# Recurrence of an RWKV branch: scaled keys of both groups of heads ahead of their products, products deferred and bound together

## The chip, the cores and the metric

The kernel runs on one core of one Trainium2 chip. Its time is the device time of one launch in microseconds (us). The engines are TensorE (PE in the profile, its weight loads PEld), VectorE (DVE), ScalarE (ACT), GpSimd (POOL) and SyncE (SP), of which the last only issues transfers here. GpSimd's queue issues transfers too.

## The reference: what is computed

The reference runs two transformer blocks in float32 over 512 tokens of width 1024. The first block has an attention layer and a recurrent layer; the change lies in the recurrent layer. This layer multiplies its normed input (512 latent and 256 context tokens) by `rec_w_in`, runs an RWKV branch (8 heads of 64) and a long-convolution branch ("hyena") beside each other, and multiplies both, gated, by `rec_w_out`. The RWKV branch, cut and condensed to what matters:

```
def rwkv_features(u, w0, w_up, a0, a_up, k_k, k_a):
    r, k, v, dw_f, dw_b, da_f, da_b = split_cols(u, RWKV_SPLITS)
    kk = normalised(k * k_k)                                  # per head
    for d, (dw, da) in enumerate(((dw_f, da_f), (dw_b, da_b))):   # two directions
        w_log = -softplus(-(w0[d] + tanh(dw) @ w_up[d])) - 0.5
        decay = exp(-exp(w_log));  a = sigmoid(a0[d] + da @ a_up[d])
        k_d = k * (1 + (a - 1) * k_a);  b_d = kk * a

def wkv_scan(s0, r, decay, k, v, kk, b, reverse, emit):
    def step(s, inp):
        r_t, w_t, k_t, v_t, kk_t, b_t = inp
        sa = einsum('bhij,bhj->bhi', s, kk_t)
        s = s * w_t[:, :, None, :] - sa[..., None] * b_t[:, :, None, :] + v_t[..., None] * k_t[:, :, None, :]
        y = einsum('bhij,bhj->bhi', s, r_t) if emit else None
        return s, y
```

The scan runs forward and backward, over the context first and then from its state over the latent tokens; the two results are added, normalised per head (`rwkv_readout`), and a bonus term r * k * r_k * v is added.

## The kernel before, in words

It is written in a tile language: pools with a number of buffers per name, and a scheduler that sets each engine's order from priorities (the place in the program, moved by `high_priority`) and from what is ready by its own estimate. Waits between engines, and for a buffer's last reader, follow from that. So the written order is not the built order, and both matter below.

The scan is done in windows of 128 tokens, two of context and four of latent tokens, each for both directions d at once (direction 1 runs through the windows from the other end), in two groups h of four heads, and in two chunks of 64 tokens per window. For each window there are these pieces of work:

- `decays(o, d, h)`, four times a window: TensorE's "lora" products (line 1153, `mm<-lora,wu`) into a tile of the pool mm2, which has one buffer; ScalarE's tanh into `ta` and `G` (1159); GpSimd's `kd` and `G` (1162, 1164); VectorE's running sum over G (1166); ScalarE's exponentials; GpSimd's kd product; for latent windows a store of kd from SyncE's queue (1176); VectorE's ta (1177), KR, and the scaled keys kT (1184), by the tiles ta, kd and G. `ta` has one buffer, `kd` and `G` have two, `kT` one for each direction.
- `products(o, d, h, kT)`, four times a window: eight products of keys (1198, `mm<-KR,kT`) into another tile of the same mm2 buffer; ScalarE takes N from it (lines 1206 and 1208), VectorE AK (1211) and, in latent windows, DD (1213); then four transposes of kT on TensorE into the PSUM tile "tr" (1219), which ScalarE copies to kn (1220).
- `invert`: VectorE's inversion of all four N of the window, 62 small operations between the transposes 1321 and 1336, and products on TensorE behind it (1351, 1353).
- `steps(o, c, VU)`: the recurrence over one chunk (lines 1387 to 1415), a chain through TensorE, VectorE and ScalarE.

`prep(o, h)` is two decays and then two products, of one group of heads. The loop over the six windows i writes: steps of chunk 0 of window i, inversion of window i + 1, steps of chunk 1, prep of window i + 2 for h = 0 and then h = 1, values of window i + 1.

Around this chain the scheduler lays work that is independent of it: `late()` is `values()` (products of the weights for v and r), `rest()` (the weight products for the gates and the convolution's inputs; priorities set by `at` as fractions of the stage), `rwkv_bonus`, `conv` (the convolution; its first lines, the transform's tables `tab` (1623) and its spectrum `K` (1644), are loaded by SyncE), and `rwkv_out` (normalisation of the result, lines 1479 to 1490, in two halves). Weight products (lines 114 to 116) take three TensorE products per block, with the weights split into a high and a low part: `wraw` is loaded by SyncE, ScalarE makes `whi` (108), VectorE `wlo` (109). Behind the stage stand the products with `rec_w_out`, whose weights go the same way. `hl` and `yl` (2472) are the low parts of their other factor.

## Time and profile before

| | |
|---|---|
| Median of 3 runs | 2869.42 us (2861.07 to 2869.76) |
| The profiled execution's own time | 2864.4 us |
| Its span in the trace | 2861.5 us |
| Mean granted TensorE clock | 0.951 |
| TensorE busy | 2645.9 us, 92% of the span |
| VectorE busy | 1495.3 us, 52% |
| ScalarE busy | 1028.4 us, 36% |
| GpSimd busy | 503.8 us, 18% |

A row of the table by windows gives a stretch in us from the start of the span, then the busy time of each engine in it with its number of instructions, then the granted clock of TensorE (1.00 is full speed), the busy share of the DMA engines and GB/s. A row in order of time gives the start, the duration, engine, line, operation, out<-in, shapes and count; in square brackets stands the idle time of the engine just before it and what released it. A row by line gives busy time, mean duration in ns, and the idle time ahead with its releasers. TensorE's products overlap their neighbours in the pipeline, so their durations add up to more than the time between their starts. The recurrence's stage lies between 755 and 1290 us of the span.

### The profile page before, as it was taken

The page shows a single profiled execution, that of the slowest core. Times are in us where ns is not written, and L with a number is a line of the kernel's source. Part 1 is how long each engine was busy: PE and PEld are TensorE (multiplying, and loading weights), DVE is VectorE, ACT ScalarE, POOL GpSimd, SP SyncE. Part 2 cuts the span into 40 slices and gives each one's busy share as a digit, 9 for nine tenths or more (in the row PEclk, how much of TensorE's full clock was granted, in tenths as well). Part 3 has the DMA queues.
Part 4 walks back from the last instruction along what each step waited for, and adds up shares of the span by engine and source line. Part 5 has one row for each costly group of instructions (what it writes and reads, how often), then busy time and mean ns, then how long its engine had stood idle before and what let it go on. Part 6 is the DMA issues. An engine that isn't in the chain of part 4 may idle for free.

```text
span 2861.5 us, 43340 instructions
## 1 busy us (share of the span) xinstructions
PE 2645.9 (92%) x16642; PEld 2125.4 (74%) x16642; DVE 1495.3 (52%) x3219; ACT 1028.4 (36%) x2165; POOL 503.8 (18%) x803
## 2 busy tenths in 40 slices
PE   8998998989989889878999998999989999899998
PEld 5897445678767666658888877777868776888887
DVE  4144557736487888685344237762232566444423
ACT  4223335524344444223333224432222663323322
POOL 1011001222343332432000001311010344100000
PEclk9999899989899899988999998999987999999999
DMA  6111431142223332524333323232453315233332
GB/s 231 60 60 55 145 119 63 57 129 81 83 87 113 90 93 66 174 94 138 96 96 96 96 85 108 83 96 91 122 160 104 106 55 161 89 100 100 96 96 88
DMA packets 251018, 290.60 MB, mean 102 GB/s; under 512 B 17415, under 2 KB 197082, under 8 KB 250812
## 3 DMA queue, kind: packets, MB, share of 16 engines
q1 hardware_dynamic: 239292, 251.29, 28.4%
q0 software_dynamic: 10704, 33.41, 3.9%
q8 instruction: 131, 2.15, 0.3%
q10 hardware_dynamic: 816, 3.15, 0.3%
q14 instruction: 75, 0.61, 0.1%
HBM read 247.38 MB, written 35.68 MB: 99 GB/s over the span
## 4 chain that ended last, share of the span: by engine, by line
PE 71%; DVE 11%; issue 5%; POOL 5%; DMA 4%; ACT 3%; SPq 0%; DVEq 0%; POOLq 0%; ACTq 0%
PE mm L114 13%; PE mm L115 13%; PE mm L116 13%; PE gt L114 3%; PE gt L115 3%; PE gt L116 3%; PE ac L116 1%; PE ac L115 1%; PE ac L114 1%; PE ac L874 1%; PE fx L333 1%; PE ac L2053 1%; PE mm L813 1%; DVE wlo L109 1%; PE tr L857 1%
## 5 line engine op out<-in xcount | busy, mean ns | idle before, releaser
L109 DVE TENSOR_TENSOR wlo<-wraw,whi 128x512 fp32r<-128x512 f32 (+1 forms) x390 | 374.5, 961 | 690.1 <-ACT whi L108 683.3
L108 ACT ACTIVATE whi<-wraw 128x512 fp32r<-128x512 f32 (+1 forms) x390 | 323.7, 831 | 792.5 <-PE mm L115 224.3
L114 PE MATMUL mm<-hh,whi 128*128 128x512 f32 (+1 forms) x1024 | 384.0, 376 | 1.0 <-ACT hh L178 0.7
L115 PE MATMUL mm<-hl,whi 128*128 128x512 f32 (+1 forms) x1024 | 383.5, 375 | 0.0
L116 PE MATMUL mm<-hh,wlo 128*128 128x512 f32 (+1 forms) x1024 | 383.0, 374 | 0.1
L114 PEld LDWEIGHTS mm<-hh,whi 128*128 128x128 f32 x1024 | 193.8, 190 | 35.7 <-ACT hh L178 1.3
L116 PEld LDWEIGHTS mm<-hh,wlo 128*128 128x128 f32 x1024 | 193.5, 189 | 35.2 <-DVE wlo L109 1.2
L115 PEld LDWEIGHTS mm<-hl,whi 128*128 128x128 f32 x1024 | 193.9, 189 | 33.1
L114 PE MATMUL mm<-whi,mh 128*128 128x512 f32 (+1 forms) x480 | 172.4, 360 | 1.4 <-DVE th L2270 1.4
L115 PE MATMUL mm<-wlo,mh 128*128 128x512 f32 (+1 forms) x480 | 173.0, 360 | 0.1
L116 PE MATMUL mm<-whi,ml 128*128 128x512 f32 (+1 forms) x480 | 172.7, 360 | 0.0
L114 PE MATMUL gt<-hh,whi 128*128 128x512 f32 (+1 forms) x320 | 128.7, 402 | 7.0 <-ACT whi L108 6.4
L116 PE MATMUL gt<-hh,wlo 128*128 128x512 f32 (+1 forms) x320 | 128.3, 401 | 0.8 <-DVE wlo L109 0.8
L115 PE MATMUL gt<-hl,whi 128*128 128x512 f32 (+1 forms) x320 | 127.6, 399 | 0.0
L283 POOL TENSOR_TENSOR ss<-sq 128x1 f32<-128x1 f32 x8 | 1.6, 201 | 707.3 <-ACT th L277 707.3
L114 PE MATMUL mm<-lath,whi 128*128 128x512 f32 (+1 forms) x280 | 116.4, 417 | 0.1
L116 PE MATMUL mm<-lath,wlo 128*128 128x512 f32 (+1 forms) x280 | 113.7, 407 | 1.0 <-DVE wlo L109 1.0
L115 PE MATMUL mm<-latl,whi 128*128 128x512 f32 (+1 forms) x280 | 113.3, 405 | 0.4 <-DVE latl L179 0.4
L114 PEld LDWEIGHTS mm<-whi,mh 128*128 128x128 f32 x480 | 89.9, 188 | 15.8 <-DVE th L2270 1.8
L115 PEld LDWEIGHTS mm<-wlo,mh 128*128 128x128 f32 x480 | 90.1, 188 | 14.4 <-DVE wlo L109 0.8
L116 PEld LDWEIGHTS mm<-whi,ml 128*128 128x128 f32 x480 | 90.1, 188 | 13.8
L114 PEld LDWEIGHTS gt<-hh,whi 128*128 128x128 f32 x320 | 62.2, 194 | 21.7 <-ACT whi L108 7.4
(732 smaller groups left out, 5987.7 us busy)
## 6 DMA issues: line engine op xcount, KB each, us to landing
wraw<-in_ffn_w_gate SPq DMA_DIRECT2D x44, 512.0 KB, 3.5
wraw<-in_ffn_w_up SPq DMA_DIRECT2D x44, 512.0 KB, 3.6
wraw<-in_ffn_w_down SPq DMA_DIRECT2D x44, 512.0 KB, 3.7
wraw<-in_w_in SPq DMA_DIRECT2D x60, 256.0 KB, 2.8
wraw<-in_rec_w_in SPq DMA_DIRECT2D x58, 256.0 KB, 2.8
wraw<-in_attn_w_in SPq DMA_DIRECT2D x26, 512.0 KB, 3.7
ada_w<-in_rec_ada_w SPq DMA_DIRECT2D x24, 512.0 KB, 3.7
wraw<-in_w_branch_gate SPq DMA_DIRECT2D x48, 256.0 KB, 3.0
```

The source lines that it names most:

```text
L108: nc.scalar.activation(hi, raw, AF.Copy)
L109: self.weng.tensor_sub(lo, raw, hi.bitcast(F32))
L114: mm(out, lh, rh, start=start, stop=False)
L115: mm(out, lh, rl, start=False, stop=False)
L116: mm(out, ll, rh, start=False, stop=stop)
L283: nc.gpsimd.tensor_add(ss, sq[:, i, 0:1], sq[:, i, 1:2])
L333: nc.tensor.matmul(p[o:o + 32], self.cs[:, kk], w[:, k], start=kk < 4, stop=kk >= 4, tile_position=(0, o))
L813: nc.tensor.matmul(ps[p][:, o:o + n], qaT[heads[p], pr, 128 * i:128 * i + 128], ks[p], start=True, stop=True)
L857: nc.tensor.transpose(t[:, j * 128:j * 128 + 128], s[:, a:a + 128], b.ident)
L874: nc.tensor.matmul(o[heads[p], xs], va[rows, n, h * 64:h * 64 + 64], pT[rows, p, j, xs], start=j == 0, stop=j == nk - 1)
L2053: nc.tensor.matmul(o, r["v"][br][:, j], pT[br][:, j].rearrange("p a b -> p (a b)"), start=False, stop=br == 1 and j == i)
```

## The change

Of the two groups of heads of a window, all four `decays` are written first, and then all four `products`; before, each group's two products stood behind its own two decays. In `products`, the first of the eight key products is given a later place (`late_by`, 0.6 of the priorities that one turn of the loop takes; 0 for the first two windows), and the other seven and the four transposes are bound to follow it on TensorE (`issue_after`), with the priority set back. The tiles change with it: kT gets two buffers per direction, kd one instead of two, and the raw weights of `values()` two instead of three. The line numbers behind this place shift by 9 or 10.

```diff
-        with tc.tile_pool(name="rv_w", bufs=1, side="right") as work, b.weights(side="right", size=512):
+        with tc.tile_pool(name="rv_w", bufs=1, side="right") as work, b.weights(raw=2, side="right", size=512):
...
-            kd = wp.tile([128, 2, H], F32, name="kd", bufs=2)
+            kd = wp.tile([128, 2, H], F32, name="kd")
...
-            kT = wp.tile([128, 2, 2, 2, 64], F32, name=f"kT{d}")
+            kT = wp.tile([128, 2, 2, 2, 64], F32, name=f"kT{d}", bufs=2)
...
+            todo = list(itertools.product(range(2), repeat=3))
+            with tc.high_priority(offset=-late_by[0]):
+                first = part(*todo[0])
+            kn = w3.tile([128, 2, 2, 128], F32, name=f"kn{d}")
+            pt = b.psum(512, "tr")
+            with tc.high_priority(offset=late_by[0]), tc.issue_after(first.ins):
+                for x in todo[1:]:
+                    part(*x)
+                for c in range(2):
+                    for pr in range(2):
                         m = 2 * c + pr
...
+                        nc.tensor.transpose(pt[:, m * 128:m * 128 + 128], kT[:, pr, c].rearrange("p x t -> p (x t)"), b.ident)
...
-        def prep(o, h):
+        def scaled(o, h):
...
-            kT = [decays(o, d, h) for d in range(2)]
-            for d in range(2):
-                products(o, d, h, kT[d])
+            return [decays(o, d, h) for d in range(2)]
+
+        def prep(o):
...
+            kT = [scaled(o, h) for h in range(2)]
+            for h in range(2):
+                for d in range(2):
+                    products(o, d, h, kT[h][d])
...
         for i in range(6):
+            q0 = tc.cur_priority
...
-            prep_of(i + 2, 0)
-            prep_of(i + 2, 1)
+            late_by[0] = int(0.6 * (tc.cur_priority - q0))
+            prep_of(i + 2)
```

TensorE's built order in the first window, from the lora products of the second round of decays on (x4 stands for four instructions of the kind in a row, mm_7437 and so on are tiles of mm2 or of weight products), before:

```order
L1153 MATMUL mm_7437<-lora,wu 128x128 x4
L115 MATMUL mm<-latl,whi 128x512
L116 MATMUL mm<-lath,wlo 128x512
L114 MATMUL mm<-lath,whi 128x512
L115 MATMUL mm<-latl,whi 128x512
L116 MATMUL mm<-lath,wlo 128x512
L114 MATMUL mm<-lath,whi 128x512
L1219 MATMUL tr<-ident,kT_7429 128x128 x4
L115 MATMUL mm<-latl,whi 128x512
L116 MATMUL mm<-lath,wlo 128x512
L1198 MATMUL mm_7462<-KR_7427,kT_7429 128x64 x8
```

and after:

```order
L1153 MATMUL mm_7437<-lora,wu 128x128 x4
L115 MATMUL mm<-latl,whi 128x512
L116 MATMUL mm<-lath,wlo 128x512
L114 MATMUL mm<-lath,whi 128x512
L115 MATMUL mm<-latl,whi 128x512
L116 MATMUL mm<-lath,wlo 128x512
L114 MATMUL mm<-lath,whi 128x512
L115 MATMUL mm<-latl,whi 128x512
L116 MATMUL mm<-lath,wlo 128x512
L114 MATMUL mm<-lath,whi 128x512
L115 MATMUL mm<-latl,whi 128x512
L1153 MATMUL mm_7469<-lora,wu 128x128 x4
```

Before, the transposes of the first round's keys and their products stand six and eight weight products behind the second round's lora products; after, ten weight products and then the lora products of the third round stand there, and products and transposes come later.

SyncE's queue at the end of the stage, where the tables of the convolution's transform (tab), its spectrum (K), its gates and the stores of the bonus term are issued, before:

```order
L1623 DMA tab_12646<-in_k_hyf 128x512
L1644 DMA K<-d_spec 128x4x256 x2
L1682 DMA gate<-d_hy 128x512 x3
L1461 DMA d_bonus<-k_11639 128x512
L1461 DMA d_bonus<-k_11654 128x512
L1623 DMA tab_12648<-in_k_hyf 128x512
```

and after:

```order
L1653 DMA K<-d_spec 128x4x256 x2
L1691 DMA gate<-d_hy 128x512 x3
L1632 DMA tab_12646<-in_k_hyf 128x512
L1632 DMA tab_12648<-in_k_hyf 128x512
L1632 DMA tab_12650<-in_k_hyf 128x512
L1632 DMA tab_12652<-in_k_hyf 128x512
L1470 DMA d_bonus<-k_11624 128x512
```

The four tables stood on both sides of two bonus stores, one ahead and three behind; now all four stand ahead of the first store that comes behind the gates.

VectorE at the very end of the stage, from the last z of the convolution to the low part (wlo) of the first block of the output weights, before:

```order
L1692 SCALAR_TENSOR_TENSOR z_12641<-z_12641,gate 128x512
L1490 SCALAR_TENSOR_TENSOR ctxh<-ctxh,g 128x2x128
L2472 TENSOR_TENSOR hl<-z_12640,hh 128x512
L2472 TENSOR_TENSOR hl<-z_12641,hh 128x512
L2472 TENSOR_TENSOR yl<-ctxh,yh 128x2x128 x4
L109 TENSOR_TENSOR wlo<-wraw,whi 128x1024 x2
```

and after, the eleven rows ahead of that wlo and wlo itself; the last z (1701) stands 25 rows ahead of it:

```order
L1498 SCALAR_TENSOR_TENSOR ctxh<-ctxh,v_gn_w,bn 128x2x128
L1497 TENSOR_TENSOR ctxh<-ctxh,iv 128x2x128
L1499 SCALAR_TENSOR_TENSOR ctxh<-ctxh,g 128x2x128
L1497 TENSOR_TENSOR ctxh<-ctxh,tr 128x2x128
L2481 TENSOR_TENSOR yl<-ctxh,yh 128x2x128
L1498 SCALAR_TENSOR_TENSOR ctxh<-ctxh,v_gn_w,bn 128x2x128
L2481 TENSOR_TENSOR yl<-ctxh,yh 128x2x128
L1499 SCALAR_TENSOR_TENSOR ctxh<-ctxh,g 128x2x128
L1498 SCALAR_TENSOR_TENSOR ctxh<-ctxh,v_gn_w,bn 128x2x128
L2481 TENSOR_TENSOR yl<-ctxh,yh 128x2x128
L1499 SCALAR_TENSOR_TENSOR ctxh<-ctxh,g 128x2x128
L109 TENSOR_TENSOR wlo<-wraw,whi 128x1024
```

Between that z and the first wlo stood one row of the normalisation (ctxh), two hl and four yl; now the four hl, five small operations of the per-head scale, the whole normalisation of the last tokens (ctxh, lines 1497 to 1499, which are 1488 to 1490 of before, four of each) and three yl stand there.

## Rows read from the trace of the kernel before

**Rows 1.** By windows: stretch, busy PE, PEld, DVE, ACT, POOL; clock; DMA.

```profile
755.00:1150.00 395.00, 350.02 (x3750) 270.06 (x3750) 312.58 (x780) 172.23 (x389) 139.68 (x243) 0.92 0.30 88
1150.00:1300.00 150.00, 121.49 (x784) 93.75 (x784) 105.16 (x189) 35.31 (x72) 58.63 (x61) 0.90 0.46 150
```

**Rows 2.** Transposes by line, 750 to 1160 us: busy, ns, idle.

```profile
L1219 PE MATMUL tr<-ident,kT 128*128 128x128 f32 x96 | 17.9, 314 | 31.1 <-DVE kT L1184 22.9 <-DVE inv_t L1331 5.0 <-ACT whi L108 3.0
```

**Rows 3.** TensorE in order of time: start, us, what, idle before.

```profile
905.03 1.16 PE L1198 MATMUL mm<-KR,kT 64*128 64x128 f32 x16 [0.64 <-DVE DD L1213]
909.43 0.72 PE L1153 MATMUL mm<-lora,wu 32*128 32x128 f32 x8
...
913.24 0.40 PE L114 MATMUL mm<-lath,whi 128*128 128x512 f32 x1
913.47 0.39 PE L115 MATMUL mm<-latl,whi 128*128 128x512 f32 x1
916.00 0.66 PE L1219 MATMUL tr<-ident,kT 128*128 128x128 f32 x4 [2.13 <-DVE kT L1184]
```

**Rows 4.** VectorE in order of time, the same stretch.

```profile
907.23 0.69 DVE L1211 TENSOR_TENSOR AK<-mm,k_rwmask 64x512 f32<-64x512 f32 x1 [2.35 <-ACT N L1208]
...
915.53 0.41 DVE L1184 TENSOR_TENSOR kT<-kd,G 128x256 f32<-128x256 f32 x1
...
921.63 0.41 DVE L1184 TENSOR_TENSOR kT<-kd,G 128x256 f32<-128x256 f32 x1
```

**Rows 5.** A gap on TensorE, and a window behind it.

```profile
765.75 0.63 PE L1219 MATMUL tr<-ident,kT 128*128 128x128 f32 x4 [1.89 <-DVE kT L1184]
...
770.00:775.00 5.00, 5.00 (x18) 3.45 (x18) 2.25 (x5) 1.97 (x6) 1.91 (x4) 0.50 0.39 132
```

**Rows 6.** Waits of VectorE, 755 to 1156 us: us, times, longest.

```profile
DVE ta L1177 <- POOL kd L1162: 21.6, 19, 5.9
DVE AK L1211 <- ACT N L1208: 14.5, 10, 2.8
```

**Rows 7.** Ends of two inversions on VectorE, in order of time.

```profile
1027.58 1.16 DVE L1336 STREAM_TRANSPOSE inv_n<-inv_x 128x512 f32<-128x512 f32 x1
...
1141.63 1.12 DVE L1336 STREAM_TRANSPOSE inv_n<-inv_x 128x512 f32<-128x512 f32 x1
```

**Rows 8.** Table by windows, columns as in rows 1.

```profile
1183.79:1282.90 99.11, 83.45 (x404) 64.11 (x403) 85.69 (x150) 23.07 (x51) 40.37 (x33) 0.91 0.26 85
1028.00:1089.20 61.20, 52.58 (x694) 40.12 (x693) 51.87 (x130) 27.90 (x68) 22.94 (x40) 1.00 0.32 93
```

**Rows 9.** DMA by line: size of one, median us to landing.

```profile
tab<-in_k_hyf SPq DMA_DIRECT2D x4, 256.0 KB, 6.4
...
d_kb<-kd SPq DMA_DIRECT2D x16, 128.0 KB, 1.8
wraw<-in_rec_w_in SPq DMA_DIRECT2D x51, 256.0 KB, 2.8
```

**Rows 10.** SyncE's queue in order of time, end of the stage.

```profile
1157.63 0.42 SPq L1620 DMA_DIRECT2D z<-d_hy  x1
...
1177.29 2.31 SPq L1623 DMA_DIRECT2D tab<-in_k_hyf  x3
```

**Rows 11.** VectorE in order of time, end of the stage.

```profile
1183.79 0.42 DVE L1656 TENSOR_TENSOR C<-M,mm 128x256 f32<-128x256 f32 x1 [1.32 <-ACT M L1655]
...
1287.79 1.22 DVE L109 TENSOR_TENSOR wlo<-wraw,whi 128x1024 fp32r<-128x1024 f32 x1 [2.02 <-ACT whi L108]
```

**Rows 12.** VectorE by line, 1156 to 1284 us: busy, ns, idle.

```profile
L1489 DVE SCALAR_TENSOR_TENSOR ctxh<-ctxh,v_gn_w,bn 128x256 f32<-128x256 f32 x8 | 4.8, 604 | 0.1
...
L2472 DVE TENSOR_TENSOR hl<-z,hh 128x512 fp32r<-128x512 f32 x4 | 2.6, 681 | 0.0
```

**Rows 13.** Table by windows, columns as in rows 1.

```profile
1156.00:1174.00 18.00, 13.83 (x141) 8.58 (x139) 6.24 (x14) 4.28 (x8) 6.44 (x10) 1.00 0.95 318
1174.00:1177.00 3.00, 0.53 (x10) 0.53 (x12) 1.35 (x3) 0.00 (x0) 0.79 (x2) 0.88 0.11 44
```

More of the change, by code (lines that the diff above doesn't have):

```diff
@@ L1192, in products, with part @@
             ps = b.mm2.tile([128, 2, 512], F32, name="mm2")
-            for c in range(2):
-                for pr in range(2):
-                    for q in range(2):
-                        qs = slice(64 * q, 64 * q + 64)
+            def part(c, pr, q):
+                qs = slice(64 * q, 64 * q + 64)
+                m = 2 * c + pr
+                return nc.tensor.matmul(ps[:, q, m * n:m * n + n], kT[qs, pr, c].rearrange("p x t -> p (x t)"),
+                                        KR[qs, pr, c, 0:n // 64].rearrange("p x t -> p (x t)"), start=True, stop=True)
+            todo = list(itertools.product(range(2), repeat=3))
[8 more added lines that the diff above has]
+                    for pr in range(2):
                         m = 2 * c + pr
-                        nc.tensor.matmul(ps[:, q, m * n:m * n + n], kT[qs, pr, c].rearrange("p x t -> p (x t)"),
-                                         KR[qs, pr, c, 0:n // 64].rearrange("p x t -> p (x t)"),
-                                         start=True, stop=True)
+                        nc.tensor.transpose(pt[:, m * 128:m * 128 + 128], kT[:, pr, c].rearrange("p x t -> p (x t)"), b.ident)
             pv = ps[:, :, 0:4 * n].rearrange("p q (m x t) -> p q m x t", m=4, t=64)
@@ L1213, in products @@
                 nc.vector.tensor_tensor(by(o["DD"][h][:, d]), pv[:, :, :, 1], bc(mask[:, 1 + d], 128), op=OP.mult)
-            kn = w3.tile([128, 2, 2, 128], F32, name=f"kn{d}")
-            p = b.psum(512, "tr")
-            for c in range(2):
-                for pr in range(2):
-                    m = 2 * c + pr
-                    nc.tensor.transpose(p[:, m * 128:m * 128 + 128], kT[:, pr, c].rearrange("p x t -> p (x t)"), b.ident)
-            nc.scalar.activation(kn.rearrange("p c r f -> p (c r f)"), p, AF.Copy, scale=rsc[:, d:d + 1])
+            nc.scalar.activation(kn.rearrange("p c r f -> p (c r f)"), pt, AF.Copy, scale=rsc[:, d:d + 1])
             o["kn"][h].append(kn)
@@ L1269, in invert, with prep_of @@
             o["T"] = unit_inverse(b, wp, bp, o["N"], (64, 0), "iv")
-        def prep_of(i, h):
+        def prep_of(i):
             if i < 6:
-                if h == 0:
-                    ws.append(window(i))
-                prep(ws[i], h)
-        ws, ST, Y = [], [None, None], None
-        prep_of(0, 0)
-        prep_of(0, 1)
+                ws.append(window(i))
+                prep(ws[i])
+        ws, ST, Y, late_by = [], [None, None], None, [0]
+        prep_of(0)
         invert(ws[0])
-        prep_of(1, 0)
-        prep_of(1, 1)
+        prep_of(1)
         Y = late()
```

## The prediction

> **What bounds the kernel now.** The diff moves instructions only inside rwkv, so I looked first for where that lies in time. In the built order the engines leave the old order near 755 us of the trace and are back in it near 1290 us; everything outside is the same, so only these 535 us can change. The table by windows [rows 1] gives two stretches: 755 to 1150 us, where TensorE is busy for 350.02 of 395 us at a granted clock of 0.92, and 1150 to 1300 us, where VectorE with 105.16 of 150 us is nearly as busy as TensorE.
>
> Next I read TensorE's waits [rows 2]: the largest is that of the transposes of the scaled keys, line 1219, for VectorE's kT: 31.1 us of idle time over 24 groups, 22.9 us of it directly for kT. One of them [rows 3]: TensorE goes on with weight products behind the lora products of 909.43 us, comes to the transposes early and stands 2.13 us. VectorE's rows of the same time [rows 4] show why: the last kT multiplication of the second direction (921.63 us) comes 6.1 us after that of the first (915.53 us), because ta has one buffer and each round goes through ScalarE, GpSimd and VectorE. That loop of 6.1 us is what TensorE is late by. A gap can also cost clock: between 770 and 775 us, behind one of 1.89 us, the granted clock was 0.50, the lower of its two levels [rows 5].
>
> These waits look like the whole prize. But VectorE's own waits [rows 6] are mostly for GpSimd and ScalarE (ta for kd 21.6 us, AK for N 14.5 us), not for TensorE, and the inversions set the pace: a window's inversion starts (line 1321) when its four groups of products are in N, and ends with line 1336. The last two rounds, from end to end 1027.58 to 1141.63 us [rows 7], take 114 us; in the first of them VectorE is busy 51.87 of 61.20 us [rows 8]. VectorE paces the steady part, and TensorE fills its gaps with weight products.
>
> **The change part by part.** Number and size of the instructions are equal before and after. The sum is made against the profiled execution, 2864.4 us, which is 5.0 us under the median of the runs.
>
> Transposes and products later. The 31.1 us of [rows 2] go, since the first product of a group now stands behind weight products or recurrence steps, and the transposes follow the products. But four rounds of decays now stand in a row. The third lora product needs the only mm2 buffer back, thus the second round's tanh, thus ta, thus the first round's kT. With the order printed above, the third comes after ten weight products, 0.23 us apart (913.24 and 913.47 us), and the second's own 0.72 us [rows 3]: 3.0 us, where the loop asks for some 5.5. In the first window I so get waits of 2.5, 2.5 and 3.2 us (third, fourth, first product), 8 us, against a mean of 5.2 us a window that goes. In the second I get 6 us; in the other four recurrence steps stand between the lora products, and I take 0 to 3 us for each. That is about 20 us in sum, with bounds 0 (the steps cover all) and 31 (the lateness only changes its place); 20 us for some ten waits is nearest to the single wait of 2.13 us [rows 3]. TensorE gets back about 11 us.
>
> The products bound together. They share mm2 with each other: product, N on ScalarE, AK and DD on VectorE, then the next product. From a product's start (905.03 us) to its AK (907.23) is 2.2 us and AK takes 0.69 us [rows 3, 4], DD as long, so a round is at least 3 us, and in 11 of the 18 gaps within a window VectorE has less than 2.4 us of other work. Its waits for N, 14.5 us now, become 14 to 22 us. The loop through ta meets less than 1.2 us of other work in 16 of 23 places, 12 of 23 before: up to 5 us more. Against that its waits for what TensorE releases, some 5 us, shrink. Between the inversions there is less to do, inside them more; the sum of VectorE's work from the first inversion to the last stays. One gain is left in front: the first window's products have 12 us less weight work ahead of them, of which 8 us go in waits, so the first inversion starts some 4 us earlier. The last inversion ends 4 us earlier, with bounds -14 and +6.
>
> kd with one buffer. The next write of kd waits for the last kT and for the store of kd. The store lands in 1.8 us [rows 9], the loop takes 6.1, and the write follows a tanh that already waits for that kT, so nothing; if SyncE's queue holds the store back, up to 1 us in each of 16 rounds. Weight buffers from 3 to 2 in values(): a block feeds TensorE for some 4 us (its products 0.23 us apart) and loads in 2.8 us [rows 9], so nothing, at worst 2 us.
>
> The end of the stage. Before, three of the transform's tables are queued on SyncE behind two stores of the bonus, until 1177.29 us [rows 10]; its first result on VectorE starts at 1183.79 us [rows 11], 42.2 us after the last line 1336 [rows 7]. In the changed order the tables stand ahead of these stores, and the last weight product, which frees their memory, stands ahead of the last inversion's first product. K loads then start some 8 us after line 1336, behind the last gate store, as they do now; nine issues of 0.42 us [rows 10] and 6.4 us to land [rows 9] make it 18 us, and the first result 20 us: 22 us earlier. From there to the last z VectorE is busy 85.69 of 99.11 us [rows 8]; nearly the same work is left there, and I add 5 us for the recurrence's hops in between. But behind that z the order now holds the whole normalisation of the last tokens ahead of the first weights' low part: four each of lines 1488, 1489 and 1490, four hl, three yl and five small operations, at 0.4 to 0.7 us each [rows 12] 11.3 us of work where it was 4.0, and a round through TensorE and ScalarE of 2 us. The first wlo (1287.79 us, [rows 11]), 4.9 us behind the end of the last z now, comes some 9 us later, and TensorE, which needs it, with it. That makes -22 + 5 + 9 = -8; since the bonus loads compete for the same time I take -7, with bounds -20 and +5.
>
> The Trainium skill, "Trainium Kernel Development and Optimization", section Key Constraints, bears on this place: transfers issued from any engine's queue run on the same 16 DMA engines and interleave, so spreading them over queues saves only issue time. By that, the tables gain only what those engines leave idle.
>
> The rows on it: from 1156 to 1174 us the DMA engines are 0.95 busy at 318 GB/s, from 1174 to 1177 they stand at 0.11 [rows 13]. If the bytes alone decide, the tables gain 3 us and little more, not 22. That is rival two.
>
> The sum is -4 - 7 = -11 us: 2853 for the profiled execution, 2858 beside the median.
>
> **The rivals.** One, a larger gain: the waits of [rows 2] do pace the stage, and the clock goes with them. The clock of 0.92 over 395 us [rows 1] is 32 us lost, and I lay 25 us of it to such waits, as the one of [rows 5]. Half of 31 + 25 comes back, and 12 us at the end: -40, 2829. For it speaks that TensorE has the highest busy share; against it, the rounds of [rows 7, 8].
>
> The Trainium skill, "TensorE: Matmul & The Clock Gate", section HAM oscillation, would have it so: gaps between bursts are paid for again and again in clock. The trace agrees that low clock follows such gaps [rows 5], and no row shows what it costs where VectorE sets the pace.
>
> Two, no change: the transfers of 1156 to 1174 us set the start of the transform, whatever the queue's order, and the normalisation at the end eats the little that is gained: -4 + 2, 2867.
>
> Three, slower: the four rounds of decays in a row, at VectorE. If each of 23 passages through ta costs 1.5 us, ta's 21.6 us become 35, and bound products make AK's 14.5 us 22: 21 us more in the queue that paces the inversions, less 4 in front and 7 at the end: +10, 2879. It decides where the waits for ta and AK, 36 us together [rows 6], grow by more than 11. Against it: inversion steps stand between these instructions in most windows.
>
> That the change doesn't do what it says is excluded for the order: the rows printed above show the groups as described.
>
> **How the numbers follow.** Forecast 0.45, rival one 0.15, two 0.20, three 0.20. A measurement of this kernel tells about 0.3% (8.6 us) from no change. Of the forecast, whose bounds together are -25 and +5, 0.33 lies beyond -8.6 us, 0.11 within, 0.01 above; rival one is all faster; two divides into 0.03, 0.15 and 0.02; three into 0.03 within and 0.17 slower. That makes 0.51 faster, 0.29 the same (with rounding), 0.20 slower. The range runs from rival one's middle, 2830, to rival three's, 2880, and leaves out half of either.
>
> **What the changed profile would show.** Idle time before the transposes under 3 us; instead some 20 us before lora products and first products, released by ScalarE's tanh. The last line 1336's counterpart at about 1138 us. The transform's first result on VectorE about 20 us behind it. The first wlo of the output weights some 14 us behind the end of the last z. The forecast is wrong if the lora products don't wait and the rounds between inversions shorten (rival one), if the transform's first result is over 35 us behind the inversion (two), or if VectorE's waits for ta and AK pass 47 us (three).

## The result, and the profile after

The changed kernel is slower: a median of 2881.02 us (2878.25 to 2889.95, 8 runs) beside 2859.82 us (2854.64 to 2869.76, 8 runs) of the kernel before on the same chip, a ratio of 1.0069 (95% interval 1.0049 to 1.0090). The forecast was 2858 us with a range of 2830 to 2880. The profiled execution of the changed kernel took 2887.9 us, with a span of 2886.1 us: 24.6 us more than the span of before. The median of 2869.42 us from which the forecast was made was that of the first 3 runs.

First the table by windows, the same two stretches as [rows 1] (stretch, busy time of TensorE, its weight loads, VectorE, ScalarE, GpSimd; granted clock; DMA share and GB/s):

```profile
755.00:1150.00 395.00, 348.67 (x3443) 265.71 (x3441) 296.71 (x716) 164.30 (x377) 137.67 (x236) 0.88 0.30 86
1150.00:1300.00 150.00, 129.10 (x985) 98.94 (x984) 110.51 (x217) 31.88 (x66) 56.17 (x59) 0.86 0.35 120
```

In the first stretch VectorE has done 296.71 us of work where it had done 312.58: it is behind by 16 us, and TensorE, as busy as before, has executed 3443 instead of 3750 instructions at a clock of 0.88 instead of 0.92.

Where it falls behind is seen at the ends of the inversions (VectorE in order of time, line 1345, which was 1336; the answer to [rows 7]):

```profile
1043.56 1.05 DVE L1345 STREAM_TRANSPOSE inv_n<-inv_x 128x512 f32<-128x512 f32 x1
...
1169.80 1.06 DVE L1345 STREAM_TRANSPOSE inv_n<-inv_x 128x512 f32<-128x512 f32 x1
```

They were at 1027.58 and 1141.63 us. The path from mark to mark, with the difference to before at each (ends of instructions; of the transform's first result and of wlo the starts):

| Mark | before, us | after, us | behind |
|---|---|---|---|
| end of inversion 1 | 833.9 | 833.9 | 0.0 |
| of inversion 2 | 878.0 | 882.6 | 4.6 |
| of inversion 3 | 977.1 | 985.4 | 8.3 |
| of inversion 4 | 1028.7 | 1044.6 | 15.9 |
| of inversion 5 | 1089.1 | 1104.8 | 15.7 |
| of inversion 6 | 1142.8 | 1170.9 | 28.1 |
| transform's first result | 1183.8 | 1193.9 | 10.1 |
| last z of the convolution | 1282.9 | 1304.3 | 21.4 |
| first wlo of the output weights | 1287.8 | 1317.7 | 29.9 |

So the inversions lose 28.1 us, the stage's end as a whole 1.8 us, and behind the stage the profiled execution makes 5.3 us good, in code that is the same in both.

Most of the loss, 23.5 of the 28.1 us, lies between the second and the sixth inversion. One window of that stretch for each kernel, before and then after, columns as above:

```profile
878.00:1142.80 264.80, 234.09 (x2794) 177.85 (x2792) 214.17 (x537) 115.99 (x263) 85.12 (x151) 0.94 0.30 87
```

```profile
882.60:1170.90 288.30, 258.19 (x2813) 192.71 (x2811) 219.09 (x539) 116.89 (x266) 86.48 (x151) 0.90 0.28 80
```

VectorE's work is nearly the same (214.17 and 219.09 us, 537 and 539 instructions); its idle time is 50.6 us before and 69.2 us after. TensorE stands idle as long as before, 30.7 and 30.1 us. What VectorE waits for is in its waits over these stretches (what waits, for what; us in total, times, longest). Those on TensorE of before:

```profile
DVE VU L1397 <- PE ru L1368: 2.3, 3, 1.9
DVE Rs L1394 <- PE ru L1392: 0.9, 2, 0.7
DVE ST L1413 <- PE ru L1406: 0.8, 1, 0.8
```

and of after:

```profile
DVE Rs L1403 <- PE ru L1401: 10.1, 6, 2.7
DVE ST L1422 <- PE ru L1415: 5.5, 6, 2.0
DVE VU L1406 <- PE ru L1377: 4.6, 4, 1.7
DVE AK L1221 <- PE iv L1270: 2.7, 2, 1.9
```

The rows by Rs, ST and VU are links of the recurrence's chain. Before, VectorE hardly ever waited for TensorE in it (4.0 us); now it waits 20.2 us there, and 23.9 us with all rows of the view on TensorE. The waits that the prediction watched did not grow over the whole path: from 755 us to the last inversion ta for kd has 20.9 us (21.6 in [rows 6]) and AK for N 15.0 us (14.5).

The last round shows one way in which an inversion comes late. TensorE in order of time: the products of the last window's groups (line 1198 before, 1196 after) and the first product of the previous inversion (1351, now 1360). Before:

```profile
1080.89 1.16 PE L1198 MATMUL mm<-KR,kT 64*128 64x128 f32 x16 [0.17 <-ACT G L1159]
1087.71 0.94 PE L1198 MATMUL mm<-KR,kT 64*128 64x128 f32 x12
1089.19 1.20 PE L1351 MATMUL iv<-inv_n,N 32*32 32x32 f32 x64 [0.55 <-DVE inv_n L1336]
...
1101.21 2.08 PE L1198 MATMUL mm<-KR,kT 64*128 64x128 f32 x16
1107.19 1.16 PE L1198 MATMUL mm<-KR,kT 64*128 64x128 f32 x16 [0.24 <-ACT xt L569]
```

After:

```profile
1104.84 1.92 PE L1360 MATMUL iv<-inv_n,N 32*32 32x32 f32 x64 [1.75 <-DVE inv_n L1345]
...
1116.48 1.16 PE L1196 MATMUL mm<-KR,kT 64*128 64x128 f32 x16
1122.85 1.16 PE L1196 MATMUL mm<-KR,kT 64*128 64x128 f32 x16
1126.67 1.16 PE L1196 MATMUL mm<-KR,kT 64*128 64x128 f32 x16
1130.72 1.16 PE L1196 MATMUL mm<-KR,kT 64*128 64x128 f32 x16
```

Before, two of the four rounds came while VectorE was still busy with the previous inversion, and two were left behind it; now all four stand behind it, four to six us apart, with weight products and the recurrence's between them on TensorE. VectorE, in order of time in that stretch of after (start, duration, line, idle time ahead in brackets), has not enough else to do:

```profile
1122.71 0.42 DVE L1403 COPY Rs<-ru 128x256 f32<-128x256 f32 x1 [2.68 <-PE ru L1401]
1125.06 0.69 DVE L1221 TENSOR_TENSOR AK<-mm,k_rwmask 64x512 f32<-64x512 f32 x1 [1.93 <-ACT N L1218]
...
1128.89 0.68 DVE L1221 TENSOR_TENSOR AK<-mm,k_rwmask 64x512 f32<-64x512 f32 x1 [1.51 <-ACT N L1218]
...
1133.19 0.69 DVE L1221 TENSOR_TENSOR AK<-mm,k_rwmask 64x512 f32<-64x512 f32 x1 [1.45 <-ACT N L1218]
...
1135.23 1.98 DVE L1330 STREAM_TRANSPOSE inv_n<-N 128x1024 f32<-128x1024 f32 x1
```

The last inversion starts 30.4 us behind the end of the one before it, where it was 21.6.

But this is the last round and not all four. In sum, from the second inversion's end to the sixth's, the time between the end of one inversion and the start of the next is 109.4 us before and 110.4 after. What grows is the time from an inversion's start to its end: 155.4 us before, 177.9 after, with VectorE idle in it for 14.3 and 28.8 us (36.3 and 40.4 us between the inversions). The built order lays steps of the recurrence between the operations of an inversion, and VectorE stands there until TensorE has made their products. Such a wait in the last inversion, first on VectorE, then what TensorE did in it:

```profile
1141.79 0.24 DVE L1342 TENSOR_TENSOR inv_x<-inv_x,inv_t 128x78 f32<-128x78 f32 x1
1144.31 0.42 DVE L1403 COPY Rs<-ru 128x256 f32<-128x256 f32 x1 [2.27 <-PE ru L1401]
1144.65 0.25 DVE L1340 TENSOR_TENSOR inv_t<-inv_n,inv_x 128x100 f32<-128x100 f32 x1
```

```profile
1142.26 0.43 PE L1401 MATMUL ru<-diag,KR 128*64 128x128 f32 x2
1142.62 0.50 PE L116 MATMUL mm<-lath,wlo 128*128 128x512 f32 x1
1143.05 0.43 PE L1401 MATMUL ru<-diag,KR 128*64 128x128 f32 x2
1143.41 0.49 PE L114 MATMUL mm<-lath,whi 128*128 128x512 f32 x1
1143.84 0.43 PE L1401 MATMUL ru<-diag,KR 128*64 128x128 f32 x2
```

After every two of the recurrence's products stands a weight product. Three of VectorE's waits for TensorE, 6.3 us together, are of this kind; two more, 3.6 us, fall into a stretch (1010 to 1017 us) in which the granted clock was 0.53.

On TensorE the change does what it set out to do. Its groups by line, 750 to 1180 us (busy, mean ns, idle ahead and releasers), beside [rows 2]:

```profile
L1196 PE MATMUL mm<-KR,kT 64*128 64x128 f32 (+1 forms) x384 | 29.0, 291 | 13.0 <-ACT G L1159 4.1 <-DVE DD L1223 3.5 <-DVE AK L1221 3.2
L1153 PE MATMUL mm<-lora,wu 32*128 32x128 f32 x192 | 24.1, 320 | 11.4 <-ACT G L1159 11.1 <-DVE AK L1221 0.3
L1210 PE MATMUL tr<-ident,kT 128*128 128x128 f32 x96 | 17.5, 307 | 0.0
```

The transposes (1210) have no idle time ahead of them any more, where they had 31.1 us; the lora products and the products of keys have 24.4 us.

At the end of the stage, VectorE in order of time and the window between, beside [rows 11] and the first of [rows 8]:

```profile
1193.91 0.42 DVE L1665 TENSOR_TENSOR C<-M,mm 128x256 f32<-128x256 f32 x1 [1.24 <-ACT M L1664]
...
1317.66 1.23 DVE L109 TENSOR_TENSOR wlo<-wraw,whi 128x1024 fp32r<-128x1024 f32 x1 [0.44 <-DVE ctxh L1499]
```

```profile
1170.90:1193.90 23.00, 18.65 (x202) 13.30 (x203) 6.19 (x9) 6.00 (x11) 10.69 (x18) 0.56 0.92 329
1193.91:1304.30 110.39, 94.70 (x612) 73.74 (x612) 90.32 (x154) 23.17 (x51) 45.47 (x42) 0.91 0.27 88
```

The transform's first result comes 23.0 us behind the last inversion instead of 41.0, with the DMA engines 0.92 busy in between; from there to the last z it takes 110.4 us instead of 99.1, and from there to the first wlo 13.4 us instead of 4.9. What moved is the start of the loads, as SyncE's queue shows, before and then after, at the first of the convolution's z:

```profile
1156.57 0.32 SPq L1620 DMA_DIRECT2D z<-d_hy  x1
```

```profile
1169.33 0.32 SPq L1629 DMA_DIRECT2D z<-d_hy  x1
```

That is 13.8 us behind the last inversion's end before and 1.6 us ahead of it after. From this issue to the first result it takes 27.2 us before and 24.6 after.

### The profile page after: what moved, and what is told of

Read it like the earlier page. It is cut to its first block, busy times and chain, and to the rows that moved or that the text cites. A ratio compares the mean times of both kernels' runs of the same rounds, so it can differ in the third digit from the quotient of the medians.

```text
span 2886.1 us, 43332 instructions
## 1 busy us (share of the span) xinstructions
PE 2671.1 (93%) x16642; PEld 2137.3 (74%) x16642; DVE 1499.5 (52%) x3219; ACT 1026.1 (36%) x2165; POOL 502.7 (17%) x803
## 3 DMA queue, kind: packets, MB, share of 16 engines
q1 hardware_dynamic: 239292, 251.29, 28.1%
## 5 line engine op out<-in xcount | busy, mean ns | idle before, releaser
L116 PEld LDWEIGHTS mm<-hh,wlo 128*128 128x128 f32 x1024 | 193.6, 189 | 35.4 <-DVE wlo L109 1.0
L114 PEld LDWEIGHTS mm<-whi,mh 128*128 128x128 f32 x480 | 89.9, 188 | 15.7 <-DVE th L2279 1.8
L115 PEld LDWEIGHTS mm<-wlo,mh 128*128 128x128 f32 x480 | 90.1, 188 | 14.5 <-DVE wlo L109 0.8
L116 PEld LDWEIGHTS mm<-whi,ml 128*128 128x128 f32 x480 | 90.1, 188 | 13.8
```

The costliest lines, as they stand in the source:

```text
L114: mm(out, lh, rh, start=start, stop=False)
L115: mm(out, lh, rl, start=False, stop=False)
L116: mm(out, ll, rh, start=False, stop=stop)
```

## The experiments

The change has three parts: the groups first, the lateness (late_by), and the binding; and the buffers beside them. Theories L (the lateness costs), G (four decays in a row and the groups bound), C (the clock), later T (TensorE's queue: what VectorE waits for stands behind weight products) and V (the late products' own rounds). Every ratio is to the kernel before on the same chip, with its 95% interval. Marks and windows are from the one profiled execution of each kernel, and single executions of a kernel differ by some 1% (the kernel before: 2843 to 2892 us over all of them).

**e4_groups_first**, from the kernel before:

```diff
-            kT = [decays(o, d, h) for d in range(2)]
-            for d in range(2):
-                products(o, d, h, kT[d])
+            return [decays(o, d, h) for d in range(2)]
...
+                    kT = [prep(ws[i], g) for g in range(2)]
+                    for g in range(2):
+                        for d in range(2):
+                            products(ws[i], d, g, kT[g][d])
```

> Groups first alone: four decays and then four products, which are written as before (no late place, not bound, transposes behind each one's N and AK), with the buffers of the change. Theory L: within 6 us of the kernel before. Theory G: slower by 15 us or more, with VectorE idle some 20 us longer between the second and the sixth inversion than in the kernel before. Theory C: slower only as far as the granted clock is below 0.92 there.

Measured: 2866.24 us, 0.9996 (0.9969 to 1.0022). The window from the second to the sixth inversion:

```profile
878.90:1140.40 261.50, 235.93 (x2793) 180.77 (x2791) 215.18 (x537) 116.62 (x264) 87.58 (x151) 0.93 0.30 88
```

VectorE idle 46.3 us, 4 less than before. Four rounds of decays in a row cost nothing that can be measured. Theory G falls.

**e3_buffers_only**, from the kernel before: only the buffers.

```diff
-b.weights(side="right", size=512)
+b.weights(raw=2, side="right", size=512)
...
-            kd = wp.tile([128, 2, H], F32, name="kd", bufs=2)
+            kd = wp.tile([128, 2, H], F32, name="kd")
...
-            kT = wp.tile([128, 2, 2, 2, 64], F32, name=f"kT{d}")
+            kT = wp.tile([128, 2, 2, 2, 64], F32, name=f"kT{d}", bufs=2)
```

> The kernel before with the buffers of the change alone: kd with one, kT with two per direction, the raw weights of values() with two. The prediction priced them at nothing: within 4 us of before. If the single kd or the two weight buffers cost what the prediction's bounds allowed: up to 16 us and 2 us more.

Measured: 2866.88 us, 1.0018 (0.9989 to 1.0048); last inversion's end at 1137.8 us, VectorE idle 49.2 us. No loss in the stage; the interval does not exclude one of a few us elsewhere.

**e8_bound_apart**, from e2 (below): the binding alone, `late_by[0] = 0`, groups apart, buffers of before.

> Binding alone: groups apart and buffers as before, late_by 0, but each group's eight products and four transposes bound together. Theory L: within 6 us of before. If the binding costs by itself (the 0.3% between the kernel with groups first alone and the one with groups first and bound): +5 to +12 us.

Measured: 2871.89 us, 1.0025 (1.0002 to 1.0048); VectorE idle 61.4 us, last inversion's end at 1148.2 us. A small loss, at the edge of what the measurement tells.

**e1_not_late**, from the changed kernel:

```diff
-            late_by[0] = int(0.6 * (tc.cur_priority - q0))
+            late_by[0] = 0
```

> The changed kernel with late_by held at 0: both groups' scaled keys first, products bound together, but not moved later. Theory L (the late place of the products is the cost: they stand alone behind the inversion, so that the next inversion starts late, 28 us by the last one): the last inversion ends within 8 us of the kernel before (1143 us), and with the shorter transform start (-18 us) and the longer end (+20 us) the time is within 6 us of the kernel before. Theory G (the four rounds of decays in a row and the groups bound together are the cost): it stays 15 us or more slower than before, last inversion at 1160 us or later. Theory C (low clock after gaps on TensorE is the cost): the time follows the clock; the granted clock of 830 to 1171 us is back at 0.93 where the time is back, and VectorE's waits for TensorE's recurrence products (13 us more than before in the changed kernel) stay.

Measured: 2872.76 us, 1.0034 (1.0012 to 1.0056); last inversion's end at 1148.7 us, VectorE idle 54.3 us, clock 0.94 in that stretch. Without the lateness half of the loss is gone, and most of it in the inversions. The time, some 10 us above before, is outside the 6 us that theory L allowed: groups first and bound, without lateness, cost something too, where groups first alone (e4) did not.

**e10_late_only**, from the kernel before: only the lateness, with late_by computed as in the change. Here all of products() is moved, its work on ScalarE and VectorE too; in the change only the first of the eight key products is, and the rest follows it.

```diff
             for d in range(2):
-                products(o, d, h, kT[d])
+                with tc.high_priority(offset=-late_by[0]):
+                    products(o, d, h, kT[d])
```

> The lateness alone: the kernel before, groups apart, buffers as before, products not bound, but all of products() at a place later by 0.6 of a turn. Theory L: +10 us or more, the last inversion's end at 1155 us or later. If the lateness costs only together with the groups first or with the binding: within 6 us of before.

Measured: 2886.36 us, 1.0084 (1.0053 to 1.0116); last inversion's end at 1177.2 us. Its window from the second to the sixth inversion:

```profile
880.30:1177.20 296.90, 263.59 (x2826) 196.97 (x2825) 216.30 (x540) 118.23 (x266) 84.11 (x151) 0.90 0.28 83
```

VectorE idle 80.6 us. The lateness alone, in this form, costs as much as the whole change.

**e2_groups_apart**, from the changed kernel: late and bound, with the groups apart and the buffers of before.

```diff
-            kT = [scaled(o, h) for h in range(2)]
             for h in range(2):
+                kT = scaled(o, h)
                 for d in range(2):
-                    products(o, d, h, kT[h][d])
+                    products(o, d, h, kT[d])
```

> Late and bound products alone: late_by 0.6 and the binding stay, but each group's products stand behind its own two decays again, and the buffers are those of before. Theory L: slower than before by 15 us or more, as the changed kernel is. Theory G: within 6 us of the kernel before. Theory C: between the two, with a clock of 830 to 1171 us as low as the changed kernel's 0.88.

Measured: 2876.55 us, 1.0039 (1.0019 to 1.0059); last inversion's end at 1160.9 us, VectorE idle 67.4 us. Less than theory L asked, but slower. The clock from 830 to 1171 us is 0.89, so what theory C asked for is met here too. Against the binding alone (e8, 1.0025) the lateness adds 0.14%, less than the two intervals tell apart. Of VectorE's waits in the stretch, those for TensorE are only 7.2 us here, those for ScalarE 35.4 (20.8 before): the idle time of this kernel comes another way than that of the changed one.

**e7_late_unbound**: e4 with the `high_priority(offset=-late_by[0])` of e10 around its products: groups first and late, not bound.

> Groups first and all products late by 0.6, but not bound together: products and transposes are each free to go where the scheduler puts them. Theory L (the late place alone costs): last inversion's end at 1155 to 1172 us, time +10 us or more. If the binding is needed for the loss: within 6 us of before, as with groups first alone.

Measured: 2888.02 us, 1.0080 (1.0055 to 1.0106). The window:

```profile
875.00:1159.50 284.50, 251.75 (x2807) 186.93 (x2805) 216.58 (x537) 116.22 (x265) 89.02 (x151) 0.93 0.27 81
```

As slow as the changed kernel, with VectorE idle 67.9 us, at a clock of 0.93 where before had 0.94: low clock is not needed for a loss of this size. Theory C falls as the only cause; what part the clock has in the changed kernel is taken up below.

**e5_late_30**, from the changed kernel: `int(0.3 * ...)` for `int(0.6 * ...)`.

> The changed kernel with half of the lateness (0.3 instead of 0.6). Theory L: between before and changed, +5 to +15 us. Theory G: as the changed kernel, +15 us or more. Theory C: no order with the lateness; the time goes with the clock alone.

Measured: 2882.33 us, 1.0067 (1.0041 to 1.0093); last inversion's end at 1160.6 us. Half of the lateness costs as much as all of it: theory L's size was wrong, it is no price per step.

**e11_early_30** and **e11_groups_early_30**: e10 and e7 with `int(-0.3 * ...)`, so that the products are moved earlier. **e12_prep_early_30**: the same shift for decays and products together, around both calls of prep_of.

> The opposite sign: the kernel before with products() moved 0.3 of a turn earlier (lateness -0.3), groups apart, nothing bound. Theory L, if the place of the products alone sets the inversions' starts: no slower than before, VectorE's idle time between the second and the sixth inversion at or below the 50.6 us of before. If any shift from the place of before costs (the scheduler's balance, not the lateness): +8 us or more.

> Groups first with products 0.3 of a turn earlier, nothing bound. Theory L: as groups first alone (2866 us against 2863 us of before) or faster; if any shift costs: +8 us or more.

> The kernel before with decays and products together 0.3 of a turn earlier. Theory L: no slower than before, since the inversions can start earlier still. If the decays are then in the way of the inversions and the recurrence on VectorE: +8 us or more, with longer inversions (before: 32 to 49 us each).

Measured: 2898.15 us, 1.0101 (1.0056 to 1.0146); 2877.51 us, 1.0042 (1.0011 to 1.0074); and 2933.61 us, 1.0222 (1.0180 to 1.0263). VectorE's idle time in the stretch is 81.7, 62.7 and 111.1 us, its work 215, 215 and 216 us. Theory L in its plain form falls: earlier costs too. In e11_early_30, VectorE's longest rows of waits, 880 to 1175 us, are those of the recurrence on TensorE again:

```profile
DVE Rs L1397 <- PE ru L1395: 11.9, 7, 5.4
DVE ST L1416 <- PE ru L1409: 8.5, 5, 5.4
```

With the weight products where they are, the place of the products in the kernel before is the best of those tried; every shift from it made VectorE idle for longer.

**e6_before_light** and **e6_after_light**: TensorE's load. In the ten column blocks laid around the recurrence one of three products of a block is left out:

```diff
         mm(out, lh, rh, start=start, stop=False)
-        mm(out, lh, rl, start=False, stop=False)
+        if not getattr(self, 'light', 0):
+            mm(out, lh, rl, start=False, stop=False)
         mm(out, ll, rh, start=False, stop=stop)
```

> The kernel before with one of the three products of each weight block left out in the ten column blocks laid around the recurrence (160 products of 512 columns, some 37 us of TensorE at 0.23 us each; the gates' inputs are then less exact). It is the base for the same cut of the changed kernel. Theory T (TensorE's queue paces the stage, weight products stand ahead of the recurrence's): 20 us or more faster than before. Theory V (the chain of products and VectorE's own work pace it): less than 12 us faster.

> The changed kernel with the same products left out. Theory T: the 20 us between the two kernels shrink to 8 us or less against the light kernel before, since what pushed the recurrence back is gone from TensorE. Theory V (the late products' rounds through the one mm2 buffer, with VectorE idle in them): 15 us or more are left between the two.

Measured: 2844.17 us, 0.9923 (0.9894 to 0.9951), and 2849.52 us, 0.9949 (0.9931 to 0.9968). Of the 0.69% between the two kernels 0.26% is left, 5.4 us between the medians, and the two intervals overlap. The windows from the second to the sixth inversion, light before and light after:

```profile
875.80:1121.80 246.00, 211.76 (x2657) 160.05 (x2656) 210.96 (x538) 116.76 (x265) 88.46 (x151) 0.90 0.34 100
```

```profile
873.10:1122.80 249.70, 205.22 (x2640) 155.06 (x2640) 210.97 (x538) 115.85 (x265) 85.03 (x150) 0.90 0.35 103
```

Now 3.7 us apart instead of 23.5, VectorE idle 35.0 and 38.7 us, and both at a clock of 0.90; VectorE's waits for TensorE are 6.8 and 7.8 us. The window of light before is from its slowest execution (2863.70 us), that of light after from its fastest (2843.21 us), so the 3.7 us may be too few. Theory T's expectation holds for both.

**e13_late_light** and **e13_early_light**: the same cut in e10_late_only and e11_early_30.

> The kernel with the lateness alone (+0.84% against before) with the same third of the weight products around the recurrence left out as in the two light kernels (light before: 0.9923 of before; light changed: 0.9949). Theory T (what the late products lose, they lose to weight products in TensorE's queue): 0.990 to 0.996 of before, so that less than 0.4% is left of the 0.84%. Theory V (their own rounds): 1.000 or more of before.

> The kernel with the products 0.3 of a turn earlier (+1.0% against before), with the same third left out. Theory T: 0.990 to 0.997 of before. Theory V (early products hold up VectorE by themselves, whatever else TensorE has to do): 1.000 or more.

Measured: 2863.28 us, 0.9975 (0.9950 to 1.0001), and 2848.94 us, 0.9926 (0.9903 to 0.9950). Against the light kernel before (0.9923) the early products have nothing left of their 1.0%; the late ones keep 0.52% of their 0.84%. So early products lose nothing measurable once a third of the weight products is gone. For the change as a whole more than half of the loss goes with them, by the middle values. The lateness alone met neither expectation: it lies above theory T's 0.990 to 0.996 and below theory V's 1.000, and seems to keep a loss of its own (VectorE idle 54.0 us beside 35.0), though its interval touches that of the light kernel before.

**e9_after_fill_15** and **e9_before_fill_15**, the weight products moved later instead of left out, in the changed kernel and in the one before:

```diff
-                    with at(turn / 10):
+                    with at(0.15 + turn / 10):
```

> The changed kernel with the ten column blocks of weight products around the recurrence given a place 0.15 of the stage later each, so that fewer of them stand ahead of the recurrence's and the late products on TensorE. Theory T (weight products ahead in TensorE's queue are what the late products and the recurrence wait for): the 20 us shrink to 8 us or less. Theory V (the serial rounds of the late products, with VectorE idle): 15 us or more stay.

> The kernel before with the same shift of the weight products, as the base for the shifted changed kernel. Both theories: within 8 us of before, since here the first group's products already stand ahead of the previous window's inversion; if the shift alone gains as much as in the changed kernel, it says nothing of the lateness.

Measured: 2890.13 us, 1.0101 (1.0065 to 1.0136), and 2909.94 us, 1.0182 (1.0142 to 1.0222). The shift costs by itself, where both theories had put the kernel before within 8 us: the transform, whose inputs these blocks make, starts 66.4 and 72.2 us behind the last inversion. In this pair the changed kernel is the faster one, by some 20 us, and its stretch from the second to the sixth inversion is 263.8 us where the shifted kernel before has 287.3. Theory V, which had 15 us or more of the loss stay, fails; that the sign turns was foreseen by neither. What the change gains or loses depends on where the weight products stand.

One row for each kernel of the stretch from the second inversion's end to the sixth's, VectorE's waits for TensorE in it, and where the first wlo of the output weights starts:

| Kernel | ratio | stretch, us | VectorE busy | VectorE idle | waits for TensorE | first wlo, us |
|---|---|---|---|---|---|---|
| before | 1 | 264.8 | 214.2 | 50.6 | 4.0 | 1287.8 |
| e3 buffers | 1.0018 | 262.5 | 213.3 | 49.2 | 4.7 | 1283.0 |
| e4 groups first | 0.9996 | 261.5 | 215.2 | 46.3 | 4.4 | 1294.4 |
| e8 bound | 1.0025 | 275.4 | 214.0 | 61.4 | 21.0 | 1295.3 |
| e1 groups first, bound | 1.0034 | 271.3 | 217.1 | 54.3 | 9.1 | 1297.7 |
| e2 late, bound | 1.0039 | 285.5 | 218.1 | 67.4 | 7.2 | 1304.8 |
| e10 late | 1.0084 | 296.9 | 216.3 | 80.6 | 16.3 | 1316.1 |
| e7 groups first, late | 1.0080 | 284.5 | 216.6 | 67.9 | 17.0 | 1311.1 |
| after: all three | 1.0069 | 288.3 | 219.1 | 69.2 | 23.9 | 1317.7 |
| e11 early | 1.0101 | 297.1 | 215.4 | 81.7 | 30.0 | 1327.2 |
| light before | 0.9923 | 246.0 | 211.0 | 35.0 | 6.8 | 1271.3 |
| light after | 0.9949 | 249.7 | 211.0 | 38.7 | 7.8 | 1266.2 |

VectorE's work is the same within some 8 us in all, and the stretch grows by its idle time. The time of the kernel goes with the stretch only roughly: e2 and e7 have the same stretch, and ratios of 1.0039 and 1.0080. In e2 and e10 the larger part of the added idle time is not a wait for TensorE.

## Why the prediction was wrong, step by step

- **What bounds the stage: half right.** That VectorE paces the steady part and TensorE fills its gaps was read from 51.87 of 61.20 us [rows 8], the round in which VectorE is busiest; over all four rounds it is idle for 50.6 of 264.8 us. The light kernel before contradicts the second half: with a third of the weight products gone, nearly the same VectorE work takes 246.0 instead of 264.8 us. TensorE's queue was part of the pace all along, only not visible as idle time of TensorE.
- **The transposes' 31.1 us: right, and worth nothing.** They went, and 24.4 us before lora products and products of keys came (20 were forecast). TensorE's idle time in the stretch stayed at 30 us, so the 11 us that TensorE should have got back were not there. The longer stretch went to 22 more weight products (445 instead of 423, 5 us at 0.23 us each) and to 14 us more of low clock.
- **The products bound together, and the last inversion: this step failed.** The prediction had VectorE's waits for N and ta as the only price, and "its waits for what TensorE releases, some 5 us, shrink". They grew, in the stretch from 4.0 to 23.9 us, and N and ta stayed over the whole path. The last inversion ended 28.1 us later, not 4 us earlier, outside the bounds of -14 and +6. The 4 us in front did not come either: the first inversion ends at 833.9 us in both. The sum had a term for each wait that the products would meet and none for what the recurrence's steps then wait for on TensorE, with weight products between their own. That VectorE's work moves from between the inversions into them was right (8 us); that it stands idle there, 14.5 us more, was not in the sum. Which part of the change does this is shown in part: groups first and the buffers cost nothing measurable, the binding 0.25% alone (e8), the lateness 0.84% in the form of e10, and without its lateness the changed kernel keeps 0.34% (e1). None of the signs that the prediction named for being wrong appeared, since none watched VectorE's waits for TensorE; only the last inversion's end, forecast at 1138 us, gave it away. The bounds of -25 and +5 for the sum are narrower than those of its two parts, which add up to -34 and +11; +20 lies outside both.
- **kd with one buffer, two weight buffers: nothing, as forecast** within what e3 tells (1.0018, 0.9989 to 1.0048).
- **The end of the stage: the pieces near, the sum not.** Forecast -22, +5 and +9; measured -18.0, +11.3 and +8.5: +1.8 us instead of -8. Of the -18.0 us, 15.4 are the earlier start of the loads, which the prediction had (K 8 us behind line 1336; it was issued at 1175.53 us, 5.7 behind line 1345). From the last inversion to the first wlo it takes 145.0 us before, 146.8 after, 154.0 in e4 and 138.9 in e10. An earlier transform start is in part given back before the last z: in e10 it comes 30.2 us sooner behind the last inversion than before, and the way to the last z is 18.3 us longer. The piece that was mis-sized is the recurrence's rest and the normalisation, 11.3 instead of 5 us.
- **Rival two** had the transform's start held by the bytes. That holds better than the 18.0 us let it seem: the DMA engines were 0.92 busy up to the first result, and counted from the first load of z it came 2.6 us sooner, about the 3 us that this rival gave to the tables. What it had wrong is the start of these loads, and "whatever the queue's order": in e2 and e10, whose tables stand ahead of K and the gates, the first result comes 14.9 and 17.8 us behind the first load of z. The Trainium skill, "Trainium Kernel Development and Optimization", section Key Constraints, has queues share the 16 engines; the trace agrees, with loads of SyncE's and GpSimd's queues running together in these 23.0 us, at 329 GB/s where [rows 13] had 318. No run had the tables' place alone.
- **Rival three** had the right sign, and +10 us for a measured +20, but by another way: it named the waits for ta and AK, which did not grow over the whole path, and the four decays in a row, which cost nothing measurable (e4). That its 2879 us is near the measured 2881 is luck: the median of before from which it was made, 2869.42 us, was 10 us above that of the 8 runs.
- **Rival one and the clock.** The lower granted clock is there, 0.90 instead of 0.94 over the stretch: 29 us lost instead of 15, summed over windows of 2.5 us. In e7 the loss is as large at 0.93, so low clock is not needed for it. In the changed kernel a part of the loss may still be the clock's. Executions of one kernel differ in it, and their times go with it: of those of the kernel before on record, the seven with a mean clock of 0.946 have a median of 2879.2 us, the 18 with 0.951 one of 2864.0 us. The eight of the changed kernel lie between 0.943 and 0.949. No run holds the clock still, so how much of the 20 us goes with it, and how much of the lower clock comes from the order, stays open.

What stays open besides: how the loss divides between lateness and binding, whose differences (0.14 to 0.38%) are near what the measurement tells; whether the lateness alone really keeps more (0.52%) than the changed kernel (0.26%) when a third of the weight products is gone; and why the loss does not grow from a lateness of 0.3 to 0.6.

## What to carry to other kernels

In this kernel, idle time of an engine that fills its gaps with independent work was not a reserve: taking it away moved the filler, and what another engine waited for then stood behind that filler in the same queue. Before moving a step, price not only the waits that it will meet itself, but also what other chains wait for on the engine on which it moves, and watch those waits in the changed profile. A place that a scheduler found is worth testing in both directions before a cost is put down to the direction, and with the filler lighter or elsewhere before it is put down to the step.

## What the runs showed of the hardware

A gap on TensorE was followed by low clock here too: in the changed kernel it stood 6.57 us ahead of the inversion's product at 1044.66 us, and the granted clock from 1045 to 1050 us was 0.50, the lower of its two levels, with TensorE busy all the time (columns as above):

```profile
1044.66 1.92 PE L1360 MATMUL iv<-inv_n,N 32*32 32x32 f32 x64 [6.57 <-DVE inv_n L1345]
```

```profile
1045.00:1050.00 5.00, 5.00 (x70) 4.13 (x65) 4.05 (x7) 1.28 (x2) 1.04 (x2) 0.50 0.29 98
```

Between executions of one kernel the mean granted clock is not the same, and the slower ones have the lower: 107 executions of the kernel before run from 2842.86 us at 0.958 to 2892.12 us at 0.942, and the six of light before run from 2835.64 us at 0.947 to 2863.70 us at 0.938.
